# Split-product matmuls that walk their columns from last to first

## Chip, cores and metric

The kernel runs on one core of a Trainium2 chip. The metric is device time in microseconds of that core: the median of the timed runs. Engines are named as in the profile: PE is TensorE's matmul, PEld its weight load, DVE VectorE, ACT ScalarE, POOL GpSimd, SP the queue that issues the DMAs.

## What is computed

Two transformer-like blocks run one after the other on one sequence of 512 tokens with 1024 features. The first has a state-space mixer (chunks of 128 tokens), grouped attention with 16 heads, a merge of the two and an MLP of width 4096; the second has a gated linear recurrence, and latent attention with 8 heads. Cut to the products that carry most of the work:

```python
proj = h @ w_in[l]                                   # 1024 -> q, k, v, xBC, z, dt, gates
merged = g_attn * (attn @ w_attn_out[l]) + g_ssd * (ssd @ w_ssd_out[l])
x = x + gate1 * (merged @ w_o[l])
ff = jnp.square(jax.nn.relu(h2 @ w_mlp1[l])) @ w_mlp2[l]
...
u = h @ w_in                                         # recurrence: 1024 -> 2 * 1280
y @ w_out                                            # its output, and that of latent attention
s = einsum("bqhd,bkhd->bhqk", qn_b, k_nope) + einsum("bqhr,bkr->bhqk", qr_b, k_rope)
```

All inputs are float32.

## The kernel before

Every large product is made as a split product. An operand is cut into a high part (rounded to the type that the kernel calls `F32R`) and a low part (what is left), by `weight` (lines 137 to 154: DMA, ACT cast on line 150, subtraction on DVE or POOL on line 153) or by `split` (lines 156 to 158). `mm3` on lines 160 to 164 then multiplies: high by high (L162), low moving by high stationary (L163), and high moving by low stationary (L164), all three added up in one PSUM tile:

```python
def mm3(self, out, lh, ll, rh, rl, start, stop):
    m = self.nc.tensor.matmul
    m(out, lhsT=lh, rhs=rh, start=start, stop=False)
    m(out, lhsT=lh, rhs=rl, start=False, stop=False)
    m(out, lhsT=ll, rhs=rh, start=False, stop=stop)
```

`lhsT` is the stationary operand, 128 columns that a weight load puts into the array; `rhs` is the moving operand, whose columns stream past it. One output column is written to PSUM for each moving column. The profile names an instruction `output<-moving,stationary`.

Two loops call `mm3`. `gemm_cm` (line 167) makes channel-major outputs: 128 channels by 512 tokens, stationary a block of weights, moving the 512 tokens of an activation (names such as `pm<-hh,wh`). `gemm_tm` (line 195) makes token-major outputs: 128 tokens by n channels, stationary 128 tokens of an activation, moving a row of weights with n columns (names such as `pm<-wh,rh`). A few more calls stand in `ssd_setup` (L383), `ssd_out` (L511), `rglru` (L1011), and in latent attention in `score` (L1196) and `mix` (L1215). In `score` the three passes of `mm3` open the sum of a score tile, and two plain matmuls on line 1198 add the rotated part; the softmax (`softmax_tile`, L717 to L725) then reads the tile with DVE and ACT.

The outputs lie in eight PSUM tiles of 128 by 512 float32: four named `pm` (pool `mm`) and four named `px`. The program is unrolled; a recording layer sets the semaphore waits, and PE, DVE, ACT and POOL each execute their instructions in the order in which they stand. PE runs far ahead with weight loads: the load for a matmul starts as the matmul ahead of it starts.

The stages in order of time, roughly: setup and the mixer to 520 us, attention to 750, the merge and its output product to 870, the MLP (L928 on) to 1235, the recurrence to 1430, latent attention to the end.

Of the kernel before, what the change touches and what calls it, by code (L numbers as in the profile page):

```python
# [11 lines left out]
PSUM = bass.MemoryType.PSUM  # L12

T = 512
# [44 lines left out]
class Build:  # L59
# [12 lines left out]
    @contextmanager  # L72
    def phase(self, nt=0, nbig=0, side="left", nw=0, nf=0, nx=0, nq=0):
        """pools that live as long as one phase: nt tiles of 2 KB, nbig of 16 KB, constants and small tiles"""
        i = self.nm("p")
        with ExitStack() as st:
            def pool(n, bufs):
                return st.enter_context(self.tc.tile_pool(name=n + i, bufs=bufs, side=side, reuse_waits="tile"))

            p = {"sm": pool("sm", 2), "c": pool("c", 1)}  # L80
            if nt:
                p["t"] = pool("t", nt)
            if nf:
                p["f"] = pool("f", nf)
            if nq:
                p["q"] = pool("q", nq)
            if nbig:
                p["big"] = pool("big", nbig)
            if nw:
                p["wr"], p["wh"], p["wl"] = [pool(x, n) for x, n in zip(("wr", "wh", "wl"), nw)]  # L90
            if nx:
                p["x"] = pool("x", nx)
            self.stack.append(p)
            yield
            self.stack.remove(p)
# [4 lines left out]
    @contextmanager  # L100
    def fills(self):
        """tiles of the work that fills gaps come from slots of their own"""
        self.tag = "f"
        yield
        self.tag = "t"
# [29 lines left out]

# [1 line left out]
    def weight(self, ap, gain=None, own=False):  # L137
        """gain [128, kt]: a factor per row of the weights; own: the parts are held in slots of the phase"""
        nc = self.nc
# [20 lines left out]
    def mm3(self, out, lh, ll, rh, rl, start, stop):  # L160
        m = self.nc.tensor.matmul
        m(out, lhsT=lh, rhs=rh, start=start, stop=False)  # L162
        m(out, lhsT=lh, rhs=rl, start=False, stop=False)  # L163
        m(out, lhsT=ll, rhs=rh, start=False, stop=stop)  # L164

    # channel-major product: out[128 channels, 512 tokens]
    def gemm_cm(self, blocks, rhs, evac, halves=0, kouter=0, gain=None):
        """blocks: list (per output tile) of lists of weight APs [128, kt, 128]; rhs(k)->(hi, lo)"""
        m = 0
# [23 lines left out]

    # token-major product: out[128 tokens, n channels]
    def gemm_tm(self, blocks, lhs, evac, n, touter=False, gain=None, group=NT):
        """blocks: list (per output block) of lists of weight APs [128, kt, n]; lhs(k)->(hi, lo);
        touter: the last block's weights are held, and its token tiles finish one after the other"""
        for b, blk in enumerate(blocks):
# [21 lines left out]

    # 1 / sqrt(ss / d + eps)
    def rstd(self, ss, d, tag, out=None):
# [31 lines left out]
    def transpose_norm(self, xt, rs, hi, lo, g=None, sh=None, key="xa"):  # L254
        """xt(t) -> [128, 1024] tokens; normalised, times g [128, 8], plus sh; channel-major parts in hi, lo"""
        nc = self.nc
# [26 lines left out]
    def half_stats(self, st, x, b, t):  # L283
        """sums of squares of one half of a token tile; after the second half, 1 / rms in st[2][:, t]"""
        nc = self.nc
        j = self.small([128, 512], "sqj")
        nc.scalar.activation(out=j, in_=x, func=AF.Square, accum_out=st[b][:, t:t + 1])
        s0, s1, r = [y[:, t:t + 1] for y in st]
        if b == 0:
            nc.gpsimd.tensor_scalar(out=s0, in0=s0, scalar1=1.0, scalar2=1024 * EPS, op0=ALU.mult, op1=ALU.add)  # L290
        else:
            nc.gpsimd.tensor_scalar(out=r, in0=s1, scalar1=s0, scalar2=1.0 / 1024, op0=ALU.add, op1=ALU.mult)
            nc.gpsimd.tensor_tensor(out=r, in0=r, in1=self.mhalf, op=ALU.pow)
# [3 lines left out]

    # softplus(x) = max(x, 0) + log1p(exp(-|x|)); log1p(u) = 2 atanh(u / (2 + u)) as a series
    def softplus(self, out, x, tmp):
# [14 lines left out]

    # ================= first block =================
    def mod_setup(self):
# [5 lines left out]
    def silu_c(self):  # L322
        """silu(c) on all partitions"""
        nc, a = self.nc, self.a
# [88 lines left out]
    def dt_product(self, ps):  # L413
        """steps, decays and their sums along a chunk; per token: tk1 = [F | G | dt_f | dt_b], tk2 = the decays of
        the states' inputs and outputs; per head: csb, F and G as [hi; lo] rows along the tokens"""
        nc, a = self.nc, self.a
        tk1, tk2 = self.tk1, self.tk2

        def evac(m, ps):
# [3 lines left out]
            for c in range(4):  # L423
# [8 lines left out]
                                           op1=ALU.mult)  # L432
            # F: sums up to and with a token; G: sums up to and without it; tot: of the whole chunk
            p = self.ps((128, 4, 64))
# [23 lines left out]
    def taps(self, ps, w, b, offs, tp=0):  # L458
        """depthwise taps along the tokens, from PSUM; w [128, n], b [128, 1]; offs: token offset of each tap"""
        nc = self.nc  # L460
# [23 lines left out]
    def xbc(self, g, i):  # L484
        """a conv'd and gated tile of one group: 4 of x, then B, then C"""
        m = g * 4 + i if i < 4 else 16 + g + 4 * (i - 4)
# [31 lines left out]
    def ssd_core(self, g):  # L518
        """a generator: the work of one group between its input and its output products"""
        nc = self.nc  # L520
# [192 lines left out]
    def softmax_tile(self, p, n, half=False):  # L713
        """p: PSUM [128, n] scores; returns normalised probabilities in SBUF"""
        nc = self.nc
# [29 lines left out]
    def qkv(self, g):  # L745
        """a generator: q, k, v of one group; per-head norm and rotation, token-major; stacks [hi; lo] of q^T, k^T"""
        nc, a = self.nc, self.a
# [51 lines left out]
    def attention(self):  # L799
# [24 lines left out]
        def output(h, po):  # L824
            # rows 0-63 carry v_hi, rows 64-127 v_lo; their sum goes to this head's half of the tile
            if h % 2 == 0:
# [127 lines left out]

    # ================= second block =================
    def rglru(self):
# [38 lines left out]
        for i0 in range(0, 10, 5):  # L995
            av, vv, ib = [], [], []
            v5 = self.pool("sm").tile([128, 5, 512], F32, tag="v5", name=self.nm("v5"), bufs=1)
            for i in range(i0, i0 + 5):
# [11 lines left out]
                for j, p in enumerate((pr, pi)):  # L1010
                    self.mm3(p, wh[:, j], wl[:, j], xh, xl, True, True)  # L1011
                # r = (1 + th) / 2, log a = -4 sp (1 + th), 1 - a^2 = tanh(-log a) (1 + a^2)
                th, ti, ty = self.t("thr"), self.t("thi"), self.t("ty")
# [10 lines left out]
                if i >= 2:  # L1024
                    product([(gin, i)])
            # sqrt(v / 16): the halves of the input gate and of the output gate
            nc.scalar.activation(out=v5, in_=v5, func=AF.Sqrt, scale=1.0 / 16.0)  # L1027
# [13 lines left out]
    def rope(self, dst_hi, dst_lo, src, cos, sin, nh):  # L1041
        """src [128, nh, 64] (PSUM or SBUF), cos, sin [128, 32]; the parts go to dst_hi, dst_lo [128, nh, 64]"""
        nc = self.nc
# [13 lines left out]
    def mla_in(self):  # L1057
# [14 lines left out]
        self.transpose_norm(lambda t: xv[:, t], self.r4, hh, hl, key="xb")  # L1072
        # compressed keys and values, compressed queries
        ck = self.c([128, 4, 320], "ck")
        # the norms' gains go into the weights
        self.gemm_tm([[a["w_dkv"][i] for i in range(4)]], lambda k: (hh[:, k], hl[:, k]),
# [59 lines left out]
        cqT = self.cqT  # L1136
        # rotated part of the queries, token-major, stacked [hi | lo], then per head [hi; lo] along the tokens
        qrt = []
# [20 lines left out]
    def mla(self):  # L1159
# [7 lines left out]
        def values(i):  # L1167
            # values of two heads, token-major: [hi | lo]
            vt = vts[i] = []
# [59 lines left out]
        for h in range(8):  # L1229
# [16 lines left out]
            if h in PO:  # L1246
                # the first heads' part of the output product fills the gaps of the last heads
                b = PO.index(h)
# [95 lines left out]
def pack(i):  # L1344
    """lays the inputs out for the kernel's loads; constants that depend on shapes alone"""
    import numpy as np
# [4 lines left out]

    def cm(w):  # [K, M] -> [M/128, 128, K/128, 128]
        k, m = w.shape
        return w.reshape(k // 128, 128, m // 128, 128).transpose(2, 1, 0, 3)

    def tm(w, nb, kt):  # [K, N] -> [N/nb, K/128/kt, 128, kt, nb]
        k, n = w.shape
        return w.reshape(k // 128 // kt, kt, 128, n // nb, nb).transpose(3, 0, 2, 1, 4)

    def col(v):  # [n * 128] -> [128, n]  # L1360
        return v.reshape(-1, 128).T
# [25 lines left out]
    o["w_attn_out"] = cm(i["w_attn_out"][0])  # L1387
    ws = i["w_ssd_out"][0].reshape(4, 4, 128, 4, 2, 128)  # g, k, p, m pair, m, j
    o["w_ssd_out"] = ws.transpose(0, 3, 2, 4, 1, 5).reshape(16, 128, 8, 128)
# [65 lines left out]
```

## Time and profile before

| | |
|---|---|
| timed runs, median (lowest to highest) | 1683.09 us (1682.07 to 1683.68) |
| profiled execution: span from first to last instruction | 1679.0 us |
| mean granted TensorE clock | 0.988 |
| PE busy, share of the span | 1601.9 us, 95% |
| PEld busy | 1285.6 us, 77% |
| DVE, ACT, POOL busy | 1130.3, 784.3, 446.0 us |
| share of 16 DMA engines | 27.7% |

A row of the profile's time line gives the start, the duration, the engine, the line, the operation and the operands. A matmul's duration runs to the modelled end of its last column, so that matmuls that follow each other overlap: their pace is read from one start to the next, not from the duration. The page gives the span of the profiled execution alone; the timed runs' median is 4.09 us above that span.

### The profile page before, as it was taken

Reading aid. Unit: us, or ns where it says so; the run is one execution under the profiler, and the core shown is the slowest. Engines: PE = TensorE matmul, PEld = TensorE weight load, DVE = VectorE, ACT = ScalarE, POOL = GpSimd, SP = SyncE. Lnnn points to the kernel's source line nnn. Section 1 sums busy time; section 2 is a strip of 40 time slices with the busy share of each in tenths; the row PEclk is TensorE's granted clock in tenths of the full one; section 3 lists DMA queues with packets and bytes.
Section 4 is the critical chain, followed back from the end, with each engine's and each line's share of the span. In section 5 each row is a group of like instructions: output and inputs, shape, how many; then the busy total and the mean of one; then the engine's idle time right before and its main releaser. Section 6 shows DMA issues by size and latency. Waiting matters only on the chain. (4 is left out here: it accounts for less than half of the span.)

```text
span 1679.0 us, 20887 instructions
## 1 busy us (share of the span) xinstructions
PE 1601.9 (95%) x7696; PEld 1285.6 (77%) x7696; DVE 1130.3 (67%) x1948; ACT 784.3 (47%) x1511; POOL 446.0 (27%) x322
## 2 busy tenths in 40 slices
PE   5989999999999999999989999999989899999998
PEld 3767667677678778778879888888878777888886
DVE  7899689789869888973363343434447766757883
ACT  4357455355456666652353232323336562554552
POOL 4314235244353334321042020111131011521012
PEclk9999999999999999999999999999999999999999
DMA  7511123234213122225222232332313221322211
GB/s 253 194 58 51 63 75 126 68 100 138 69 64 103 55 82 88 88 90 162 89 76 85 91 101 90 99 98 90 113 51 105 87 78 53 100 77 65 68 63 51
DMA packets 50649, 153.54 MB, mean 91 GB/s; under 512 B 8178, under 2 KB 12914, under 8 KB 50547
## 3 DMA queue, kind: packets, MB, share of 16 engines
q1 hardware_dynamic: 50546, 152.22, 27.7%
q8 instruction: 60, 0.98, 0.2%
q14 instruction: 43, 0.34, 0.1%
HBM read 150.10 MB, written 2.10 MB: 91 GB/s over the span
## 5 line engine op out<-in xcount | busy, mean ns | idle before, releaser
L150 ACT CAST wh<-wr 128x1024 fp32r<-128x1024 f32 (+5 forms) x245 | 239.7, 979 | 426.0 <-PE pm L163 192.9
L153 DVE TENSOR_TENSOR wl<-wr,wh 128x1024 fp32r<-128x1024 f32 (+2 forms) x170 | 199.6, 1175 | 220.0 <-ACT wh L150 219.7
L153 POOL TENSOR_TENSOR wl<-wr,wh 128x1024 fp32r<-128x1024 f32 (+3 forms) x75 | 175.2, 2336 | 555.2 <-ACT wh L150 521.3
L162 PE MATMUL pm<-hh,wh 128*128 128x512 f32 x432 | 174.8, 409 | 8.4 <-ACT hh L157 6.6
L163 PE MATMUL pm<-hl,wh 128*128 128x512 f32 x432 | 176.9, 409 | 2.5 <-POOL hl L158 2.4
L164 PE MATMUL pm<-hh,wl 128*128 128x512 f32 x432 | 174.0, 403 | 0.0
L944 POOL TENSOR_TENSOR r<-r 128x512 f32<-128x512 f32 x32 | 50.6, 1583 | 264.7 <-ACT r L943 264.7
L162 PE MATMUL pm<-h,wh 128*128 128x512 f32 (+1 forms) x288 | 106.9, 373 | 0.0
L164 PE MATMUL pm<-h,wl 128*128 128x512 f32 (+1 forms) x288 | 106.8, 371 | 0.0
L163 PE MATMUL pm<-h,wh 128*128 128x512 f32 (+1 forms) x288 | 106.7, 371 | 0.0
L162 PEld LDWEIGHTS pm<-hh,wh 128*128 128x128 f32 x432 | 81.8, 190 | 31.7 <-ACT hh L157 7.7
L163 PEld LDWEIGHTS pm<-hl,wh 128*128 128x128 f32 x432 | 81.9, 190 | 26.5 <-POOL hl L158 5.4
L162 PE MATMUL pm<-wh,rh 128*128 128x512 f32 x256 | 99.7, 389 | 0.0
L164 PE MATMUL pm<-wh,rl 128*128 128x512 f32 x256 | 99.6, 389 | 0.0
L163 PE MATMUL pm<-wl,rh 128*128 128x512 f32 x256 | 99.6, 389 | 0.0
L725 POOL TENSOR_SCALAR pr<-pr,psum 128x512 f32<-128x512 f32 x64 | 64.7, 1021 | 130.1 <-DVE psum L721 72.0
L164 PEld LDWEIGHTS pm<-hh,wl 128*128 128x128 f32 x432 | 82.0, 190 | 21.4 <-issue 3.1
L472 DVE SCALAR_TENSOR_TENSOR acc<-pm,conv_w_s,acc 128x510 f32<-128x510 f32 (+2 forms) x118 | 87.6, 742 | 13.0 <-ACT acc L463 12.0
L608 POOL TENSOR_TENSOR e<-e,w 128x512 f32<-128x512 f32 x32 | 52.1, 1627 | 100.9 <-ACT e L607 90.5
L251 DVE SCALAR_TENSOR_TENSOR wada<-wada,cs 128x1024 f32<-128x1024 f32 x48 | 67.2, 1410 | 14.5 <-DMA wada<-in_w_ada 14.3
L720 ACT ACTIVATE pr<-px,nmax 128x512 f32<-128x512 f32 (+2 forms) x96 | 60.4, 637 | 30.0 <-DVE nmax L717 23.9
L162 PE MATMUL pm<-ha,wh 128*128 128x512 f32 (+1 forms) x192 | 69.0, 362 | 4.7 <-DVE acc L472 4.7
(400 smaller groups left out, 4138.0 us busy)
## 6 DMA issues: line engine op xcount, KB each, us to landing
wr<-in_w_mlp SPq DMA_DIRECT2D x64, 512.0 KB, 3.5
wada<-in_w_ada SPq DMA_DIRECT2D x48, 512.0 KB, 3.9
wr<-in_w_xbc SPq DMA_DIRECT2D x24, 512.0 KB, 3.5
wr<-in_w_in_a SPq DMA_DIRECT2D x20, 512.0 KB, 3.4
wr<-in_w_z SPq DMA_DIRECT2D x16, 512.0 KB, 3.5
wr<-in_w_ssd_out SPq DMA_DIRECT2D x16, 512.0 KB, 3.4
wr<-in_w_gate SPq DMA_DIRECT2D x16, 512.0 KB, 4.0
wr<-in_w_qkv SPq DMA_DIRECT2D x16, 384.0 KB, 3.0
```

What stands on the lines that cost most here:

```text
L150: nc.scalar.copy(out=hi[:, :n], in_=raw[:, :n])
L153: eng.tensor_tensor(out=lo[:, :n], in0=raw[:, :n], in1=r32(hi[:, :n]), op=ALU.subtract)
L162: m(out, lhsT=lh, rhs=rh, start=start, stop=False)
L163: m(out, lhsT=lh, rhs=rl, start=False, stop=False)
L164: m(out, lhsT=ll, rhs=rh, start=False, stop=stop)
L251: nc.vector.scalar_tensor_tensor(out=w, in0=w, scalar=1.0, in1=self.cs, op0=ALU.mult, op1=ALU.mult, accum_out=self.modc[:, j:j + 1])
L472: nc.vector.scalar_tensor_tensor(out=acc[:, lo:hi], in0=ps[:, lo + o:hi + o], scalar=w[:, j:j + 1], in1=acc[:, lo:hi], op0=ALU.mult, op1=A ...
L608: self.e("ew").tensor_tensor(out=e, in0=e, in1=w, op=ALU.mult)
L720: nc.scalar.activation(out=e[:, :n], in_=p, func=AF.Exp, bias=nmax, accum_out=s)
L725: self.e("norm").tensor_scalar(out=e[:, :n], in0=e[:, :n], scalar1=s, scalar2=1.0, op0=ALU.mult, op1=ALU.mult)
L944: self.e("sq").tensor_tensor(out=r, in0=r, in1=r, op=ALU.mult)
```

## The change

`mm3` turns its output and both moving operands round in their column dimension: each pass reads its moving operand from the last column to the first, and writes column j of the output at the place of column j, so that the output is the same as before. The stationary operand is not touched.

```diff
     def mm3(self, out, lh, ll, rh, rl, start, stop):
         m = self.nc.tensor.matmul
+
+        out, rh, rl = out[:, ::-1], rh[:, ::-1], rl[:, ::-1]
         m(out, lhsT=lh, rhs=rh, start=start, stop=False)
         m(out, lhsT=lh, rhs=rl, start=False, stop=False)
         m(out, lhsT=ll, rhs=rh, start=False, stop=stop)
```

The rest of the diff takes out comments and docstrings. Lines below `mm3` move down by two: L162, L163 and L164 become L164, L165 and L166, L1198 becomes L1200, L720 becomes L722. All 6048 matmuls of `mm3` change; matmuls elsewhere keep their direction. No instruction is added, removed or moved on any engine, and every tile keeps its address. What moves are some semaphore waits, since the recording layer takes the overlap of two accesses otherwise when one of them runs backwards.

The first place is PE at the first product of the mixer's group after the step sizes: `pm_724` is the output, `hh` and `hl` the parts of the normalised input, `wh` and `wl` those of the weights. Before:

```order
L162 MATMUL pm_724<-hh_101,wh_726 128x512 [waits DVE_49]
L163 MATMUL pm_724<-hl_102,wh_726 128x512
L164 MATMUL pm_724<-hh_101,wl_727 128x512 [waits Pool_49]
L162 MATMUL pm_724<-hh_101,wh_726 128x512
L163 MATMUL pm_724<-hl_102,wh_726 128x512
```

and with the change:

```order
L164 MATMUL pm_724<-hh_101,wh_726 128x512 [waits DVE_49,PE_49]
L165 MATMUL pm_724<-hl_102,wh_726 128x512
L166 MATMUL pm_724<-hh_101,wl_727 128x512 [waits Pool_49]
L164 MATMUL pm_724<-hh_101,wh_726 128x512
L165 MATMUL pm_724<-hl_102,wh_726 128x512
```

The order is the same; the first pass into a reused PSUM tile now also waits for PE itself, for the matmul that last wrote that tile. Over the whole program PE's waits for itself go from 195 to 235: those on `mm3`'s first pass from 28 to 87, the others fall by 19.

The second place is ACT at the softmax of the first head of latent attention: `px` is the score tile, `nmax` the negated row maximum from DVE, `pr` the exponentials. Before:

```order
L1184 ACTIVATE qp_13054<-pm_13056 128x512 [waits PE_49]
L720 ACTIVATE pr_13083,psum_13084<-px_13074,nmax_13081 128x128 [waits DVE_49]
L720 ACTIVATE pr_13097,psum_13098<-px_13088,nmax_13095 128x256 [waits DVE_49]
L720 ACTIVATE pr_13111,psum_13112<-px_13102,nmax_13109 128x384 [waits DVE_49]
L720 ACTIVATE pr_13125,psum_13126<-px_13116,nmax_13123 128x512 [waits DVE_49]
```

and with the change:

```order
L1186 ACTIVATE qp_13054<-pm_13056 128x512 [waits PE_49]
L722 ACTIVATE pr_13083,psum_13084<-px_13074,nmax_13081 128x128 [waits DVE_49,PE_49]
L722 ACTIVATE pr_13097,psum_13098<-px_13088,nmax_13095 128x256 [waits DVE_49,PE_49]
L722 ACTIVATE pr_13111,psum_13112<-px_13102,nmax_13109 128x384 [waits DVE_49,PE_49]
L722 ACTIVATE pr_13125,psum_13126<-px_13116,nmax_13123 128x512 [waits DVE_49,PE_49]
```

ACT now waits for PE, which wrote the scores, and for DVE, which has read them since; such waits on this line go from 4 to 22 in the program.

## Rows read from the trace of the kernel before

**Rows 1.** The page: span, and busy time, share and instructions of each engine.

```profile
span 1679.0 us, 20887 instructions
...
PE 1601.9 (95%) x7696; PEld 1285.6 (77%) x7696; DVE 1130.3 (67%) x1948; ACT 784.3 (47%) x1511; POOL 446.0 (27%) x322
```

**Rows 2.** The chain that ended last, shares of the span by engine.

```profile
PE 40%; DVE 4%; ACT 2%; POOL 2%; issue 1%; POOLq 0%; DVEq 0%; ACTq 0%
```

**Rows 3.** Windows, whole span, of L162 alone: PE busy (count), PEld busy (count).

```profile
0.00:1679.00 1679.00, 765.56 (x2016) 380.58 (x2016) 0.99 0.28 91
```

**Rows 4.** Windows at 31.7, 752 and 1040 us: all engines, PEclk, DMA share, GB/s.

```profile
31.70:33.90 2.20, 2.20 (x7) 1.67 (x6) 2.10 (x7) 0.62 (x1) 0.44 (x1) 0.50 0.77 222
752.00:757.00 5.00, 5.00 (x23) 3.99 (x22) 3.45 (x3) 0.59 (x1) 1.80 (x1) 1.00 0.98 367
1040.00:1050.00 10.00, 10.00 (x46) 8.26 (x45) 2.45 (x2) 2.11 (x2) 0.00 (x0) 1.00 0.31 101
```

**Rows 5.** Time line of PE, low clock: start us, us, instruction.

```profile
31.75 0.63 PE L163 MATMUL pm<-hl,wh 128*128 128x512 f32 x1
...
33.88 0.63 PE L162 MATMUL pm<-hh,wh 128*128 128x512 f32 x1
```

**Rows 6.** Time line of PE, merge: activations moving.

```profile
752.03 0.39 PE L164 MATMUL pm<-hh,wl 128*128 128x512 f32 x1
...
754.84 0.39 PE L164 MATMUL pm<-hh,wl 128*128 128x512 f32 x1
```

**Rows 7.** Time line of PE, second MLP product: weights moving.

```profile
1040.02 0.39 PE L162 MATMUL pm<-wh,rh 128*128 128x512 f32 x1
...
1043.88 0.39 PE L164 MATMUL pm<-wh,rl 128*128 128x512 f32 x1
```

**Rows 8.** Line L162: duration ns min/median/max, first and last start, forms.

```profile
L162 PEld LDWEIGHTS pm<-hh,wh x432: 186/188/337, 21.4 to 812.2; 128*128 128x128 f32 x144
L162 PE MATMUL pm<-hh,wh x432: 388/394/1032, 21.4 to 812.5; 128*128 128x512 f32 x144
...
L162 PE MATMUL pm<-wh,rh x256: 389/389/402, 924.4 to 1232.4; 128*128 128x512 f32 x128
...
L162 PE MATMUL pm<-wh,yh x144: 387/389/628, 1377.3 to 1671.3; 128*128 128x512 f32 x144
...
L162 PE MATMUL pm<-oh,wh x64: 392/394/475, 716.9 to 818.1; 128*128 128x512 f32 x64
```

**Rows 9.** Waits of PEld for PE: us in total, times, longest.

```profile
PEld px L526 <- PE px L526: 1.0, 1, 1.0
PEld px L1153 <- PE pm L164: 0.9, 1, 0.9
PEld px L563 <- PE pm L162: 0.2, 1, 0.2
```

**Rows 10.** Groups of PE by shape, of L162: first 512 wide, then narrower; last, the narrowest.

```profile
L162 PE MATMUL pm<-hh,wh 128*128 128x512 f32 x432 | 174.8, 409 | 8.4 <-ACT hh L157 6.6 <-DVE acc L472 1.7
...
L162 PE MATMUL pm<-wh,hh 128*128 128x384 f32 x128 | 43.3, 339 | 0.0
...
L162 PE MATMUL pm<-h,wh 128*128 128x256 f32 x64 | 18.4, 297 | 0.0
...
L162 PE MATMUL pm<-wh,hb 128*128 128x320 f32 x32 | 10.0, 311 | 0.0
...
L162 PE MATMUL px<-ph,v 128*128 128x128 f32 x8 | 1.8, 224 | 0.0
```

**Rows 11.** Time line of PEld, the merge again: weight loads.

```profile
752.04 0.19 PEld L162 LDWEIGHTS pm<-hh,wh 128*128 128x128 f32 x1
752.27 0.19 PEld L163 LDWEIGHTS pm<-hl,wh 128*128 128x128 f32 x1
```

**Rows 12.** Time line of PE, 256 columns, latent attention.

```profile
1545.65 0.28 PE L164 MATMUL pm<-wh,ckT 128*128 128x256 f32 x1
...
1546.97 0.28 PE L163 MATMUL pm<-wl,ckT 128*128 128x256 f32 x1
```

## The prediction

> **What bounds the kernel now.** I read the page's busy times first: PE is busy for 1601.9 us of a span of 1679.0, VectorE for 67% [rows 1]. PE thus idles for 77.1 us in all. The chain that ended last says the same: PE holds far the largest named share, no other engine over 4% [rows 2]. So what changes the pace of matmuls changes the time, nearly one for one. Then I asked how much of PE is `mm3`: each of its three lines has 2016 matmuls, as L162 has in [rows 3]; that is 6048 of PE's 7696 [rows 1]. All of them change.
>
> The next question is what sets the pace of one. The reader should take starts, not durations. [...] In the steady streams at a granted clock of 1.00 it is more, and it is not the same everywhere: (754.84 - 752.03) / 12 = 0.234 us with activations moving [rows 6], (1043.88 - 1040.02) / 17 = 0.227 us with weights moving [rows 7]. The medians of the durations by operand show the same two levels: 394 ns for `hh` and `oh`, 389 ns for `wh` against `rh` or `yh`, beside a weight load of 188 ns in both [rows 8]. [...] The first stream also ran beside far more DMA, 0.98 against 0.31 of the engines, and more VectorE [rows 4], but the two levels hold over hundreds of matmuls elsewhere, so I put them down to the operands. This dependence is the one thing in the trace that the direction of reading could touch.
>
> **The change, part by part.** It adds and removes no instruction; the order on every engine stays. Three things can cost something.
>
> *The waits.* PE waits for itself 40 times more. Each new one is for the last writer of a reused PSUM tile, whose content another engine has since read, so it is met long before. Before, 195 such waits stand in the program, and the trace shows three stalls of this kind, 2.1 us in sum [rows 9]. I take 0. The bound above: each new wait lets the pipeline run empty, a duration of 389 ns in place of a pace of 227 [rows 7, 8], 40 x 0.162 = 6.5 us; below, nothing is gained. The new waits of ACT on line 722 are for scores that VectorE has already read: 0, with no stall to bound, since the wait for VectorE ends last.
>
> *The rate of reading and writing.* No row of the trace has a matmul that walks backwards, so its pace is bounded by the nearest rows. [...] Above: one column per period of the lower clock, 0.426 us [rows 5]. [...]
>
> *The excess of 14 to 21 ns.* Of the 6048 matmuls, 4848 have 512 columns, 528 have 384, 528 have 256, 96 have 320 and 48 have 128 (first rows of each width in [rows 10]). Groups such as `hh`, `h` and `oh` moving, 432 x 3 + 224 x 3 + 64 x 3 = 2160 matmuls, stand near 0.233 us; `wh` moving against `rh` and `yh`, 256 x 3 + 144 x 3 = 1200, near 0.227; I put the other 1488 half way. A reversed walk meets the same tiles in another phase. If it put all on the lower level: -(2160 x 6 + 1488 x 3) ns = -17 us. All on the upper level: 1200 x 6 + 1488 x 3 ns = +12 us. I take the middle of what I cannot tell, 0; both ends stay for the range.
>
> The sum is 0 us against the profiled span of 1679.0. The runs' median stands 4.09 us above that span; I carry this over, so the forecast is **1683 us**, with 1666 to 1695 for this case alone, and 1702 if all new waits cost their bound.
>
> [...]
>
> **Rivals.**
>
> *The moving read meets the weight load (slower).* Each weight load starts as the matmul ahead of it starts, at 752.04 us beside 752.03 [rows 6, 11], and takes 188 of its 227 to 234 ns [rows 6 to 8]; both read SBUF at once. For it: the pace depends on the operands, so reads do get in each other's way. If the two now run in step rather than across each other, the excess grows. If it doubles: 17 ns more on 4848 matmuls is 82 us; the narrower ones have 0.120 against 0.107 us at 256 columns [rows 12], at about 13 ns on 1200 another 16 us: 98 us, **1781 us**. It decides from the first 3.4 us, which is 0.7 ns per wide matmul. At worst the moving read goes at half rate for the whole load, which costs 94 ns in place of 17: 77 ns x 4848 = +373 us, 2056 us. Against it: nothing in the trace tells which way the load walks. [...]
>
> *One column per slow period (much slower).* If pairs of columns are fetched or written together only when they ascend, each goes alone, at 0.426 us per 512 [rows 5]. The extra is 0.426 - 0.230 = 0.196 us on the wide ones, 950 us; the others hold 528 x 384 + 528 x 256 + 96 x 320 + 48 x 128 = 374,784 columns at 0.38 ns, 142 us. Of the idle 77.1 us about half would be hidden: 1683 + 1092 - 35 = **2740 us**. Against it: the pairs stay the same pairs.
>
> *The excess goes (faster).* If the walks no longer meet, 17 ns less on 4848 is -82 us, **1601 us**. [...]
>
> [...]
>
> **How the numbers follow.** The forecast's case has 0.60, spread over -17 to +19 us: faster 0.20, within 0.2% 0.20, slower 0.20. The rival in which reads meet has 0.18, one column per period 0.13, the vanished excess 0.05, nothing at all 0.04. About 0.2%, 3.4 us, is what a measurement of this kernel can tell from no change. Faster: 0.20 + 0.05 = 0.25. Same: 0.20 + 0.04 = 0.24. Slower: 0.20 + 0.18 + 0.13 = 0.51. So the likeliest single time is the one of now, and yet slower is the likelier side, as most of the mechanisms that I can price cost time. The range leaves out one column per period and the vanished excess, 0.18 together, and of the first rival only what lies beyond 2.7 times the present excess, some 0.02: from 1664 to 1850 us. The forecast's case alone: 1664 to 1702.
>
> **What would show it.** Right: starts at 0.227 to 0.235 us in the streams of [rows 6, 7], medians of 389 and 394 ns by operand, perhaps exchanged; PE busy within 1590 to 1625 us; no stall of PE for itself above that of [rows 9]. The first rival shows as paces of 0.24 to 0.31 us for 512 columns with the granted clock at 1.00, and as more excess at 256 columns too. The second shows as 0.426 us at a granted clock of 1.00, and L1200's plain matmuls, which still walk forwards, at their old pace. The forecast is wrong if the pace of the wide ones leaves 0.225 to 0.236 us, or if PE's new waits show as idle time.

## The result, and the profile after

The changed kernel takes 1694.10 us (median of 4 runs, 1688.63 to 1697.89), the kernel before 1682.67 in the same comparison (4 runs). The ratio is 1.0065, with a 95% interval of 1.0048 to 1.0083: slower by 11.4 us, where I had forecast 1683 us and a range of 1664 to 1850.

The page of the changed kernel first: the span, the busy times and, cut out, the chain that ended last.

```profile
span 1686.8 us, 20911 instructions
...
PE 1612.7 (96%) x7696; PEld 1286.9 (76%) x7696; DVE 1127.6 (67%) x1948; ACT 784.1 (46%) x1511; POOL 444.4 (26%) x322
...
PE 40%; DVE 4%; ACT 2%; POOL 1%; issue 1%; POOLq 0%; DVEq 0%; ACTq 0%
```

Against [rows 1, 2] PE is busy for 10.8 us more, and its idle time falls from 77.1 to 74.1 us: 7.8 us more span. The chain has the same shares, but for POOL's 1% in place of 2%. So matmuls take longer; PE does not wait longer. The 24 instructions more on the page are semaphore waits (15 on ACT, 9 on PE): instructions were added after all, though none that computes. The profiled execution took 1688.63 us and was the fastest of the four.

Which matmuls, the source view of `mm3`'s first pass shows (`L164` now; durations in ns, min/median/max):

```profile
L164 PEld LDWEIGHTS pm<-hh,wh x432: 186/188/338, 20.7 to 812.7; 128*128 128x128 f32 x144
L164 PE MATMUL pm<-hh,wh x432: 394/397/802, 20.7 to 812.9; 128*128 128x512 f32 x144
...
L164 PE MATMUL pm<-wh,rh x256: 396/397/398, 924.2 to 1237.1; 128*128 128x512 f32 x128
...
L164 PE MATMUL pm<-wh,yh x144: 395/397/501, 1381.2 to 1679.1; 128*128 128x512 f32 x144
...
L164 PE MATMUL pm<-oh,wh x64: 395/398/479, 717.3 to 818.5; 128*128 128x512 f32 x64
```

The two levels of [rows 8], 394 and 389 ns, are gone: every operand is at 397 or 398. The weight load is 188 ns as before. In the time line of PE, the merge (first two rows) and the second MLP product (last two) now run at one pace:

```profile
752.03 0.40 PE L164 MATMUL pm<-hh,wh 128*128 128x512 f32 x1
...
754.83 0.40 PE L164 MATMUL pm<-hh,wh 128*128 128x512 f32 x1
...
1040.16 0.40 PE L166 MATMUL pm<-wh,rl 128*128 128x512 f32 x1
...
1043.89 0.40 PE L164 MATMUL pm<-wh,rh 128*128 128x512 f32 x1
```

(754.83 - 752.03) / 12 = 0.233 us, where [rows 6] have 0.234; (1043.89 - 1040.16) / 16 = 0.233, where [rows 7] have 0.227. The fast operands lost 6 ns each; the slow ones lost nothing. At the lower clock, too, nothing is lost:

```profile
31.49 0.63 PE L166 MATMUL pm<-hh,wl 128*128 128x512 f32 x1
...
33.20 0.63 PE L164 MATMUL pm<-hh,wh 128*128 128x512 f32 x1
```

(33.20 - 31.49) / 4 = 0.4275 us, against (33.88 - 31.75) / 5 = 0.426 in [rows 5]; the difference is the time line's rounding, as the intervals of this kind average 426.6 ns in both traces. And the waits of PEld for PE, in the view of waits, answer to [rows 9]; the last row is ACT's:

```profile
PEld px L575 <- PE pm L166: 1.4, 1, 1.4
PEld px L528 <- PE px L528: 0.9, 1, 0.9
PEld pm L164 <- PE px L1200: 0.5, 1, 0.5
PEld px L565 <- PE pm L164: 0.2, 1, 0.2
PEld pm L164 <- PE pm L166: 0.2, 1, 0.2
...
ACT pr L722 <- PE px L1200: 1.4, 1, 1.4
```

Those of PEld come to 3.2 us, against 2.1; the two on L164, 0.7 us, stand on `mm3`'s first pass, where the new waits are. ACT waits for PE on L722 once, 1.4 us, where before it did not. That these waits cost no time in the end is shown below, by a kernel that has them all and no backwards read.

**The sum.** For the pace of all operands together I averaged, in the trace, the intervals between the starts of consecutive `mm3` matmuls of equal width at the full clock, without the intervals that hold a stall (4441 before and 4460 after at 512 columns). The mean goes from 230.45 to 233.37 ns at 512 columns, from 173.54 to 176.95 at 384, and from 116.3 to 118.8 at 256; 320 and 128 stay. That is 4848 x 2.92 + 528 x 3.41 + 528 x 2.5 ns = 14.2 + 1.8 + 1.3 = 17.3 us, if all of them ran steadily. The profiled execution shows less, and pair by pair it can be placed: both programs have the same 7696 matmuls in the same order, so each interval before has its twin after. Of the pairs that are steady at the full clock in both, those that start with a wide matmul (4581) cost 13.2 us, the 384-wide 1.6 and the 256-wide 1.1: 16.0 us. The 171 pairs that touch the lower clock in either execution give back 7.5 us (the mean granted clock rose from 0.988 to 0.990), the 287 that hold a stall 1.2; matmuls outside `mm3` change by nothing, and the first matmul starts 0.4 us later. With the parts not rounded that makes the 7.8 us of span. The other three runs, at clocks of 0.984 to 0.987, have spans of 1691.4 to 1696.1 us.

### The profile page after: what moved, and what is told of

The parts are those of the page before. It is cut to its first block, busy times and chain, and to the rows that moved or that the text cites. A ratio compares the mean times of both kernels' runs of the same rounds, so it can differ in the third digit from the quotient of the medians.

```text
span 1686.8 us, 20911 instructions
## 1 busy us (share of the span) xinstructions
PE 1612.7 (96%) x7696; PEld 1286.9 (76%) x7696; DVE 1127.6 (67%) x1948; ACT 784.1 (46%) x1511; POOL 444.4 (26%) x322
## 5 line engine op out<-in xcount | busy, mean ns | idle before, releaser
L164 PE MATMUL pm<-hh,wh 128*128 128x512 f32 x432 | 175.9, 411 | 7.9 <-ACT hh L157 6.0
L165 PE MATMUL pm<-hl,wh 128*128 128x512 f32 x432 | 177.9, 412 | 2.6 <-POOL hl L158 2.6
L166 PE MATMUL pm<-hh,wl 128*128 128x512 f32 x432 | 174.9, 405 | 0.0
L166 PE MATMUL pm<-h,wl 128*128 128x512 f32 (+1 forms) x288 | 106.9, 372 | 0.0
L165 PE MATMUL pm<-h,wh 128*128 128x512 f32 (+1 forms) x288 | 106.9, 372 | 0.0
L164 PE MATMUL pm<-h,wh 128*128 128x512 f32 (+1 forms) x288 | 106.6, 372 | 0.0
L164 PEld LDWEIGHTS pm<-hh,wh 128*128 128x128 f32 x432 | 81.8, 190 | 31.2 <-ACT hh L157 7.5
L165 PEld LDWEIGHTS pm<-hl,wh 128*128 128x128 f32 x432 | 82.2, 190 | 26.4 <-POOL hl L158 5.5
L165 PE MATMUL pm<-wl,rh 128*128 128x512 f32 x256 | 101.7, 397 | 0.0
L164 PE MATMUL pm<-wh,rh 128*128 128x512 f32 x256 | 101.7, 397 | 0.0
L166 PE MATMUL pm<-wh,rl 128*128 128x512 f32 x256 | 101.7, 397 | 0.0
L727 POOL TENSOR_SCALAR pr<-pr,psum 128x512 f32<-128x512 f32 x64 | 64.6, 1020 | 130.7 <-DVE psum L723 71.1
L166 PEld LDWEIGHTS pm<-hh,wl 128*128 128x128 f32 x432 | 82.0, 190 | 21.4 <-issue 3.1
L722 ACT ACTIVATE pr<-px,nmax 128x512 f32<-128x512 f32 (+2 forms) x96 | 60.4, 636 | 30.3 <-DVE nmax L719 21.4
L164 PE MATMUL pm<-ha,wh 128*128 128x512 f32 (+1 forms) x192 | 69.0, 362 | 4.3 <-DVE acc L474 4.3
```

The costliest lines, as they stand in the source:

```text
L722: nc.scalar.activation(out=e[:, :n], in_=p, func=AF.Exp, bias=nmax, accum_out=s)
L727: self.e("norm").tensor_scalar(out=e[:, :n], in0=e[:, :n], scalar1=s, scalar2=1.0, op0=ALU.mult, op1=ALU.mult)
```

## The experiments

The tiles' places in SBUF, read from the built programs, which have them in common, gave the first theory. Nearly all weight parts lie at 96 modulo 256 bytes in their partition. The activations lie elsewhere, and the pace before sorts by the distance between the two operands, the place of the moving one less that of the stationary one, modulo 256 bytes (means of intervals as above, ns per 512 columns):

| distance | of the 4848 | operands, moving and stationary | before | changed |
|---|---|---|---|---|
| 0 | 1596 | `wh` and `rh`; `hb` and `wh` | 226.9; 227.0 | 233.5; 233.6 |
| 64 | 1020 | `ha` and `wh` | 229.1 | 233.4 |
| 32 | 672 | `h` and `wh` | 233.4 | 233.4 |
| 192 | 1488 | `hh` and `wh` | 233.0 | 233.3 |

(The other 72 are at 224.) The row of 64 is the loosest: three passes over the same tiles, `wh` with `mh` and `wl` with `mh` and `wh` with `ml`, have 229.2, 231.7 and 226.0 ns, and the 60 matmuls of `xh` and `xl` with `wgh` and `wgl` some 232. Before, distances of 0, 256, 512 and 768 modulo 1024 bytes all have 227.1 to 227.4 ns, so nothing coarser than 256 bytes is seen.

### Reading backwards alone

```diff
-        out, rh, rl = out[:, ::-1], rh[:, ::-1], rl[:, ::-1]
+        rh, rl = rh[:, ::-1], rl[:, ::-1]
```

> mm3 turns round only its two moving operands and writes its output forwards, so every product comes out mirrored in its columns (what is computed is not the reference's). Theory S: the uniform pace of the changed kernel comes from the side that reads SBUF; then 512 columns take 0.233 us from start to start with every operand, in the merge stream as in the second MLP product, and the span is that of the changed kernel, 1687 us give or take 5. Theory P: it comes from writing PSUM backwards; then the two levels of the kernel before return, 0.234 us in the merge and 0.227 in the second MLP product, and the span is 1679 give or take 3.

Measured: 1693.55 us (4 runs), ratio to before 1.0055 [1.0042, 1.0069]. The page's first line, and the source view of the first pass:

```profile
span 1693.3 us, 20887 instructions
...
L163 PE MATMUL pm<-hh,wh x432: 394/397/802, 22.0 to 817.8; 128*128 128x512 f32 x144
...
L163 PE MATMUL pm<-wh,rh x256: 396/397/398, 930.0 to 1242.9; 128*128 128x512 f32 x128
```

The whole cost and the single level of the changed kernel are there without any write that runs backwards, and with the 20887 instructions of the kernel before, so without the new waits.

### Writing backwards alone

```diff
-        out, rh, rl = out[:, ::-1], rh[:, ::-1], rl[:, ::-1]
+        out = out[:, ::-1]
```

> mm3 turns round only its output; moving operands are read forwards, so every product comes out mirrored (what is computed is not the reference's). Theory S: the pace is that of the kernel before, 0.234 us in the merge and 0.227 in the second MLP product, span 1679 give or take 3. Theory P: 0.233 us everywhere, span 1687 give or take 5. If neither run alone shows the uniform pace, it needs both.

Measured: 1682.75 us (10 runs), ratio 0.9998 [0.9989, 1.0008]. Its page's first line and its source view:

```profile
span 1680.5 us, 20911 instructions
...
L163 PE MATMUL pm<-hh,wh x432: 387/394/1068, 20.7 to 812.0; 128*128 128x512 f32 x144
...
L163 PE MATMUL pm<-wh,rh x256: 389/389/402, 923.8 to 1231.7; 128*128 128x512 f32 x128
```

Both levels of [rows 8] are back. This kernel has all the new waits, with the same 20911 instructions as the changed one, so they cost nothing that can be seen either. Walking PSUM backwards, by this ratio, costs nothing here.

### All operands at distance 0, forwards

Small pads ahead of the activations' pools, in four phases, put 4716 of the 4848 wide matmuls at distance 0, where before 1596 are. The walk is forwards.

```diff
+            if pad:
+                p["pad"] = pool("pad", 1)
+                z = p["pad"].tile([128, pad], F32, tag="pad", name=self.nm("pad"))
+                self.nc.vector.memset(z[:, 0:1], 0.0)
...
-                    A.enter_context(b.phase(nbig=3))
+                    A.enter_context(b.phase(nbig=3, pad=16))
...
-                    with b.phase(nt=NSSD):
+                    with b.phase(nt=NSSD, pad=32):
...
-                with b.phase(nt=NMLP, nbig=2):
+                with b.phase(nt=NMLP, nbig=2, pad=56):
...
-                    with b.phase(nbig=2):
+                    with b.phase(nbig=2, pad=48):
```

> The kernel before, forwards, with pads of 64 to 224 bytes ahead of four pools, so that the activations of the mixer, the attention output, the merge, the MLP and the recurrence start at the same remainder of 256 bytes as the weight tiles (before: 64 below, 32 or 64 above them). Theory S in its sharper form: the moving read and the weight load that runs beside it meet in SBUF, and how often depends on the distance of their addresses modulo 256 bytes. Then all 512-column matmuls fall to 0.227 us, also in the merge and in the first MLP product; some 2200 matmuls gain 6.5 ns and 1000 gain 2.5: -17 us, span near 1662, ratio 0.990. Rival D: the levels come from what runs beside (DMA at 0.98 of the engines in the merge, VectorE): then the merge keeps 0.234 us and the span stays at 1679.

Measured: 1672.64 us (6 runs), ratio 0.9936 [0.9920, 0.9951]: faster than both kernels. Its source view:

```profile
L166 PE MATMUL pm<-hh,wh x432: 387/389/1415, 21.8 to 812.5; 128*128 128x512 f32 x144
...
L166 PE MATMUL pm<-wh,rh x256: 389/389/389, 923.3 to 1227.3; 128*128 128x512 f32 x128
...
L166 PE MATMUL pm<-oh,wh x64: 389/389/497, 718.8 to 818.0; 128*128 128x512 f32 x64
```

All three are on the lower level now. In the merge the DMA engines and VectorE are no less busy than in [rows 4] (1.00 of the engines, and 4.76 us of 5.00), and the pace is (754.71 - 751.99) / 12 = 0.227 us all the same, so the upper level there did not come from what runs beside it:

```profile
752.00:757.00 5.00, 5.00 (x24) 4.14 (x23) 4.76 (x5) 1.85 (x2) 2.77 (x1) 1.00 1.00 379
...
751.99 0.39 PE L166 MATMUL pm<-oh,wh 128*128 128x512 f32 x1
...
754.71 0.39 PE L166 MATMUL pm<-hh,wh 128*128 128x512 f32 x1
```

The gain is 10.3 us where I expected 17: the mean at 512 columns fell by 2.73 ns, 13.2 us over 4848 (`hh` stops at 228.4, not at 226.6), and the 256-wide ones went up from 116.3 to 119.75 ns, 528 x 3.45 ns = 1.8 us given back. For them distance 0 is not the best. Not all of the 3.45 ns is the distance's, though: the control below and the kernel that writes backwards, where every distance is that of the kernel before, have 117.6.

### Other distances, and another place at the same distance

The same pads, larger by 128 bytes or by 96 in the phases of `hh`, `h` and `ha`, put those at distance 128 or 96 (the edit of the first phase, for 128):

```diff
-                    A.enter_context(b.phase(nbig=3, pad=16))
+                    A.enter_context(b.phase(nbig=3, pad=48))
```

> As the run with aligned tiles, but with the activations of the mixer, the attention output, the merge, the MLP's input and the recurrence 128 bytes past the weights' remainder of 256. Theory S: another uniform level for these 3120 matmuls, which I cannot name; between 0.220 and 0.236 us, with the rest (distance 0) at 0.227. If it is below 0.227, distance 128 is the better placement; I expect 0.229, span 1667. Rival D: as the kernel before, 1679.

Measured: 1685.88 us (10 runs), ratio 1.0012 [1.0001, 1.0023]; `hh` in its source view:

```profile
L166 PE MATMUL pm<-hh,wh x432: 388/393/1414, 21.2 to 816.9; 128*128 128x512 f32 x144
```

> As the run with aligned tiles, forwards, but with the same activations 96 bytes past the weights' remainder of 256. Theory S: a level of its own for some 2900 matmuls; by the distances seen so far (0: 0.227, 64: 0.229, 32, 128 and 192: 0.233 us for 512 columns) odd multiples of 32 are on the high level, so 0.233 us and a time of about 1686. If it is under 0.227, this distance is the better one.

Measured: 1690.5 us, one run; `hh` in its source view:

```profile
L166 PE MATMUL pm<-hh,wh x432: 388/392/1415, 21.5 to 816.5; 128*128 128x512 f32 x144
```

The means by operand are 232.5 ns (`hh`) and 233.2 (`h`) at 128, and 231.9 to 236.3 at 96. So both lie on the upper level, not at the 229 that I had expected of 128: of the distances seen, 0 stands out, and 64 lies near it. In one product, `wh` or `wl` moving against `mh` and `ml`, the pads move the stationary operand alone; the moving one keeps its place modulo 256 bytes. Its mean goes from 229.0 ns before (distance 64) to 226.8 at 0, 232.4 at 128 and 234.3 at 160. So the stationary operand's place counts, not the moving read alone.

The control is one pad ahead of all pools, which moves everything by 64 bytes and keeps the distances:

```diff
-        with b.phase(nw=NW), ExitStack() as inner:
+        with b.phase(nw=NW, pad=16), ExitStack() as inner:
```

> The kernel before, forwards, with one pad of 64 bytes ahead of all pools, so that nearly every operand of mm3 lies 64 bytes higher and every distance between moving tile and weight tile stays as it was. Theory S, distance: the levels stay, 0.234 us in the merge and 0.227 in the second MLP product, span 1679 give or take 3, time as before within 0.2%. Rival A, absolute place: the level goes with the remainder of 256 bytes of the moving tile itself; hh then lies where weights lay and falls to 0.227, weights lie where ha lay and rise to 0.229 or more: the two levels change places.

Measured: 1683.11 us (10 runs), ratio 1.0008 [0.9998, 1.0017], with both levels in place:

```profile
L166 PE MATMUL pm<-hh,wh x432: 388/394/1415, 21.0 to 815.6; 128*128 128x512 f32 x144
...
L166 PE MATMUL pm<-wh,rh x256: 389/389/402, 927.2 to 1235.1; 128*128 128x512 f32 x128
```

By this one shift, what decides is the distance of the two operands, not the place of either.

### Aligned and backwards

The pads of the aligned kernel, in the changed kernel.

> The changed kernel (backwards) with the pads of the aligned kernel, so that the activations of the split products lie at distance 0 from the weights, modulo 256 bytes. Theory that a backwards walk runs through all distances and so no longer depends on the tiles' places: every 512-wide operand at 0.233 us from start to start, merge and second MLP product alike, and a time of 1690 to 1698 us, as the changed kernel; reversal then costs about 21 us on the aligned kernel against 11 on the kernel before. Rival, that the two effects add up independently, alignment still gaining about 10 us of what reversal loses: 1680 to 1686 us and a merge at 0.228 to 0.231 us.

Measured: 1695.38 us (4 runs), ratio 1.0077 [1.0056, 1.0097]. Its source view:

```profile
L167 PE MATMUL pm<-hh,wh x432: 394/397/800, 21.9 to 818.3; 128*128 128x512 f32 x144
...
L167 PE MATMUL pm<-wh,rh x256: 397/397/398, 930.7 to 1243.6; 128*128 128x512 f32 x128
```

Alignment gains nothing here: backwards, distance 0 stands on the upper level too. The aligned kernels, forwards and backwards, were measured in different comparisons. Their medians differ by 1695.38 - 1672.64 = 22.7 us, their ratios to the kernel before by 1.0077 - 0.9936 = 0.0141, or 24 us. Either way reversal costs twice what it costs on the kernel before, since all operands now have the lower level to lose.

### A shorter weight load

Is the weight load what the moving read meets? The second pass loads 64 stationary columns in place of 128 (which leaves the low part of the moving operand out of half of the outputs), forwards and then backwards:

```diff
-        m(out, lhsT=lh, rhs=rl, start=False, stop=False)
+        n = lh.shape[1] // 2
+        m(out[:n], lhsT=lh[:, :n], rhs=rl, start=False, stop=False)
```

> The kernel before, with only 64 of the 128 stationary columns in mm3's second pass (the low part of the moving operand is left out for half of the outputs). The load for this pass runs beside the first pass. A load of 64 columns is some 54 ns shorter (134 against 188 in the kernel before). Theory S: the excess comes from the weight load's read, so the start-to-start time from first to second pass loses about half of its excess: in the merge from 0.234 to about 0.223 us, in the second MLP product from 0.227 to about 0.220; the other two steps stay. Some 1600 wide matmuls gain 7 to 10 ns: time near 1670. Rival O: the excess belongs to the moving read alone (or to the write): 0.234 and 0.227 in all three steps, time as before.

> The changed kernel with the same half-wide load in the second pass. Theory S: first to second pass about 0.223 us in place of 0.233 with every operand, the other two steps 0.233; time near 1680. Rival O: 0.233 in all three steps, time near 1694.

Measured: 1686.56 and 1693.87 us, one run each. The forward one's groups of PEld by shape, and its time line of PE in the merge:

```profile
L165 PEld LDWEIGHTS pm<-hh,wl 128*128 128x128 f32 x432 | 82.4, 191 | 42.7 <-issue 4.5
...
L164 PEld LDWEIGHTS pm<-hl,wh 128*64 128x64 f32 x432 | 58.7, 136 | 28.5 <-POOL hl L158 7.4 <-issue 3.6
```

```profile
752.71 0.40 PE L164 MATMUL pm<-ol,wh 128*64 128x512 f32 x1
752.94 0.39 PE L165 MATMUL pm<-oh,wl 128*128 128x512 f32 x1
753.17 0.39 PE L162 MATMUL pm<-oh,wh 128*128 128x512 f32 x1
753.41 0.39 PE L164 MATMUL pm<-ol,wh 128*64 128x512 f32 x1
```

The load did become shorter, 136 ns in place of 191, and the pace did not: 0.23, 0.23, 0.24 us for the three passes. The expected 0.223 failed, backwards too (0.233 in all). In the second MLP product, at distance 0, the pace even rose, from a mean of 226.9 to 228.7 on the first pass and from 227.0 to 230.5 on the second. So the pace does not follow the length of the load. That the stationary operand matters at all is shown by the distances (226.8 to 234.3 ns with its place alone); how, is open.

## Why the prediction was wrong

**What bounds the kernel: right.** PE is busy for 96% of the changed kernel's span, and its pace is the time: the kernels that read backwards, at 0.233 us, were slower (ratios 1.0055 to 1.0077), and the aligned one, which lowered the mean pace by 2.73 ns, was faster (0.9936).

**The waits, taken at 0: right.** PE's stalls for itself are 3.2 us against 2.1 and ACT's one new stall is 1.4, so the bare sign "no stall above" did not hold; but PE's idle time fell, and writing backwards alone, with the same waits, takes the time of before.

**The rate, taken as unchanged: right.** It went into the sum with 0 us. Backwards, 512 columns at the full clock take 0.233 us, not the 0.426 of [rows 5]; backwards writing costs nothing (ratio 0.9998), and at the lower clock the direction does not show (426.6 ns in both traces).

**The excess of 14 to 21 ns, "I take the middle of what I cannot tell, 0": this step failed.** The two levels were rightly found and put down to the operands, and one end of this term was what happened: "all on the upper level", +12 us, against 11.4 us of medians. That these lie so close is luck: the steady pace gives 17.3 us, because the narrower widths, which the bound left out, pay too and, with all operands averaged, the wide ones lose 2.92 ns and not 11.7 us / 4848 = 2.4. In the profiled execution the lower clock and the stalls took part of it back. The 14 to 21 ns themselves are counted from 0.213 us, half of the 0.426 us of [rows 5]: that 512 columns alone take so little at the full clock was the author's estimate, and no run shows it, nor the 0.107 us for 256 columns in the first rival; the lowest mean paces before were 226.0 ns for 512 columns, as in the pass of `wh` with `ml`, and 116.3 for 256. The two ends, -17 and +12 us, do without it, as they use the two measured levels alone. Taking the middle was the mistake: the middle was no mechanism. I could have asked what put `rh` and `yh` on the lower level, and whether a reversed walk keeps it. The places of the tiles would have told the first: a distance of 0 for just those that ran at 227 ns. For the second I have a reading that is argued, not shown: two walks in the same direction keep their distance, good or bad, while one that runs against the other passes through all distances. The sign "medians of 389 and 394 ns by operand, perhaps exchanged" fell too, as there is one level of 397.

**The carry-over of 4.09 us: right as a sum, wrong as a constant.** With the changed kernel, the time stands 1.8 us above the span (1688.63 against 1686.8). If 1.8 us is what lies around the span, the profiled execution before took some 1680.8 us, less than each of the four timed runs, and the other 2.3 us were its luck.

**The rivals.** *The moving read meets the weight load* had the right sign, and its point of decision, 0.7 ns per wide matmul, was passed with 2.92. Its price of 98 us was not: the mean pace stops at 233.4 ns, the level that `h` and `hh` already had, and a shorter load (136 ns in place of 191) does not lower it. For its premise, that the two reads get in each other's way, speaks that the pace moves from 229.0 to 226.8 or 232.4 ns with the stationary operand's place alone; no run shows the meeting itself. *One column per slow period* and *the excess goes* are excluded by the same 233.4 ns; that columns go in pairs at all, as the former supposes, no run shows. That nothing at all would change, 0.04 of the chances, is excluded by the ratio of reading backwards alone, 1.0055.

**The chances.** Slower had 0.51 and came, but 0.31 of it stood with two rivals priced at 98 and 1057 us; the case that came had 0.20.

**My own signs of right and wrong** were too coarse: "0.225 to 0.236 us" spans 11 ns x 4848 = 53 us, and the pace stayed inside it while the time moved by 11.

What stays open: whether the two reads meet, and in what way. The runs show that the distance modulo 256 bytes decides forwards (227 ns at 0, 233 at 32 and 192), that it no longer matters backwards (233.3 to 233.6 at 0, 32 and 192), and that the length of the load does not set the price (0.23 us with 136 ns as with 191). A backwards walk of the stationary operand was not tried.

## What to carry to other kernels

Where a stream of matmuls sets the time, compare start-to-start intervals by operand: here two levels at one width and one clock, 389 and 394 ns in the medians, went with the tiles' places. Where that is so, a few small pads may be worth trying: here four of 64 to 224 bytes, which put nearly all wide matmuls at distance 0 modulo 256 bytes, gained 0.64%. Reading the moving operand backwards gave that up (1695.38 us with the same pads, against 1672.64). When one term of a prediction has two known ends, ask which items stand at each end now and what would keep them there, before taking the middle.

## What was unexpected of the hardware

A 512-wide matmul at the full clock starts every 227 ns on average where moving and stationary operand lie at the same place modulo 256 bytes (228.4 for `hh` in the aligned kernel), every 229 at a distance of 64 (226 to 232 by pass and product), and every 232 to 236 at 32, 96, 128 or 192; backwards it is 233.3 to 233.6 at the distances of the table (0, 32, 64, 192). All distances tried are multiples of 32 bytes. At 256 columns distance 0 is not the best: 119.75 ns in the aligned kernel, against 116.3 before and 117.6 in two kernels with the distances of before. At the lower clock 512 columns take 426.6 ns in either direction.
